# A two-layer hybrid diffusion trunk on one core: the first norm and its products by quarters of the features, a fourth raw slot, the norm's squares by halves, and the last rows in two transfers

## The chip, the cores and the metric

The kernel runs on one NeuronCore of a Trainium2 chip. The metric is the device time of one execution in microseconds (us). The kernel before took 1372.78 us, the median of three runs (1372.05 to 1373.74).

## The reference, cut to what matters

One inference step of a backbone of two layers (`DEPTH` = 2, `D_MODEL` = 1024) in float32 on 640 tokens: 512 latent tokens (`x_sample`) and 128 context tokens (`x_prompt`). Context and latent tokens share the weights and are modulated by different vectors (`c_ctx` and `c`). A layer is:

```
m = silu(cond) @ w_ada + b_ada                  # six vectors of 1024: shift, scale, gate, twice
h = rmsnorm(x, g_pre_mix) * (1 + scale1) + shift1
pa_u, pa_v, pb_h, pb_b, pb_c, pc, pd = split(h @ w_in)       # 1888 columns; pd has 352 of them
mix = concat(chunk_mlp(pa), short_conv(pb), fourier(pc), latent_attention(pd)) @ w_out
x = x + gate1 * rmsnorm(mix, g_post_mix)
h2 = rmsnorm(x, g_pre_ffn) * (1 + scale2) + shift2
x = x + gate2 * rmsnorm(swiglu(h2, w_gate_up, w_down), g_post_ffn)
```

Outputs are `y_prompt`, `y_sample` and, for each layer, the context's normalised latents and rotary keys. The change lies in the first three lines of the first layer (their scale and shift, the norm and the 352 columns `pd`), in the norms, and in the storing of the last rows.

## The kernel before, in words

**Numbers and tiles.** The 640 tokens are five tiles of 128 (tiles 0 to 3 latent, tile 4 context). Products that need float32 accuracy are made as three matmuls of float32r operands (`mm3`, lines 227 to 229): high part by high part, high by low, low by high. So an operand is split once (`split`, lines 211 and 217): ScalarE copies the high part, rounded, and VectorE subtracts it from the source for the low part. A weight goes from memory to one of three `raw` slots (pool `rp`, 4 KB a partition each), is split into one of eight `w` slots (pool `wp`), and the raw slot is free again when VectorE has read it (`load`, line 255). Other pools are `qp` (twelve large slots), `sp` (three small slots, tag `s`), `mp` (small tiles by tag) and eight PSUM banks (`ps`).

**The order of the work.** The program is traced once, in the order of the Python code, and a scheduler then orders each engine's queue by the program's order and by what is ready in its own estimate; slots of a pool are given in that order, and a tile with no free slot waits for a release. DMA issues stand in SP's queue. Where a block stands under `manual_schedule`, the engines it names keep the order written. Beside this, the kernel has a clock of its own, `now`, which each matmul advances by its estimated length (`clk`): generators (`spawn`) yield a time, and their next part is written into the program when the clock has come that far; background steps (`bg`: the modulations of later stages, with loads of 512 KB through `raw`) are written in at fixed distances. These distances are unchanged.

**The start** (`start`, line 1291). The first modulation, scale and shift of 1024 features for two conditions, is a product of two condition columns with 8 MB of `w_ada`. It is made in two halves of 512 features. A half has four blocks of 1 MB, loaded into `qp` slots (`fetch`, line 1300); for each block TensorE makes four matmuls side by side in groups of 32 columns (`ada_mm`, line 284, eight passes in the profile), and when all four are in, `fin` copies the sums out of PSUM (ScalarE), turns them by four transposes, and adds them, the bias and the norm's weight into `mod` (VectorE). The five tiles of x are loaded and normed meanwhile (`normalise`): ScalarE squares and sums a row of 1024 (line 432), GpSimd adds epsilon and takes the power -0.5, VectorE scales the row by halves (line 435). Then, for each half of the features, four transposes a tile bring the features onto the partitions (`xnT`, line 240), `modulate` applies scale and shift out of PSUM, two blocks of 128 on ScalarE and two on VectorE (lines 211 and 464), and `split_h` splits 512 columns into `h`. The products of `pd` (`pd`, 352 columns, eight feature blocks k, three matmuls each) run in two passes over the five tiles, k 0 to 3 and then k 4 to 7, in five PSUM banks `acc`. The steps of the second half's modulation stand between the products of the first pass. The weights `w_pd` are four loads of 352 KB, two blocks k each.

**Behind it.** `pd_chain` norms the two low-rank parts of a tile of `pd` in the tile `pdt` (one slot, lines 678 to 697), waits for 6.0 of the kernel's clock, transposes it and splits the result. `mixer` follows with its own weights (`w_vpc` first, four loads), and `w_out`, `gate_up` and `w_down`; the second layer's first norm and its 352 columns are made at the end of the first layer's `w_down` by `prenorm` and `pd_all`, not by `start`. Rows of a finished tile are updated by `postnorm` in two halves (line 914). At the end of the last layer `end(t)` stores them to `y_s` or `y_p` in one transfer of 512 KB (line 1199); tile 2 is the last.

## Time and profile before

| what | value |
|---|---|
| median of 3 runs | 1372.78 us (1372.05 to 1373.74) |
| the profiled execution, its own time | 1373.93 us |
| its span | 1372.2 us |
| TensorE (PE) busy | 1331.6 us, 97% of the span, 8188 matmuls |
| VectorE (DVE) busy | 1031.7 us, 75% |
| ScalarE (ACT) busy | 694.4 us, 51% |
| GpSimd (POOL) busy | 218.5 us, 16% |
| moved by DMA | 244.08 MB |

Times in the rows below are in us from the span's start. PE is TensorE's matmuls, PEld its weight loads, DVE VectorE, ACT ScalarE, POOL GpSimd, SPq the queue from which SP issues DMAs. "L227" is line 227 of the kernel; a helper's line stands for all its callers, so groups are told apart by the tiles, written out<-in. Idle time of an engine is put down to what released it, with "<-"; a DMA is given as its target and source. A matmul's end is modelled, so matmuls that follow each other overlap in the rows.

### The profile page before, as it was taken

What the parts mean: (1) busy time and instruction counts of PE and PEld (TensorE: products, weight loads), DVE (VectorE), ACT (ScalarE), POOL (GpSimd) and SP (SyncE); (2) the same over time, 40 slices, a digit from 0 to 9 for tenths busy, and PEclk for the clock granted to TensorE, in tenths of its full rate; (3) what the DMA queues carried; (4) which work ended last, traced back from release to release, by engine and by line L of the source; (5) the groups of instructions that cost most, each with busy time, mean ns of one, the idle gap of its engine ahead of it and who ended that gap; (6) DMA issues with size and microseconds to landing.
All of it is one profiled execution on the core that took longest, in us unless ns stands there. A gap on an engine that the chain in (4) does not pass through costs nothing. (4 is left out here: it accounts for less than half of the span.)

```text
span 1372.2 us, 21590 instructions
## 1 busy us (share of the span) xinstructions
PE 1331.6 (97%) x8188; PEld 1200.3 (87%) x8188; DVE 1031.7 (75%) x1794; ACT 694.4 (51%) x1398; POOL 218.5 (16%) x306
## 2 busy tenths in 40 slices
PE   5899999999999999999999999999999999999997
PEld 2789977899999999988888997878999999998886
DVE  3789476589979976868788966757976877776875
ACT  4543276465454444656583324736545444554652
POOL 1101121111122112100121202301223112210010
PEclk9999999999999999999999999999999999999999
DMA  9555247345778567746565633554279665655653
GB/s 373 177 168 188 80 148 246 107 154 177 254 201 231 191 168 201 207 143 188 175 207 175 191 113 123 185 200 168 73 238 229 186 160 149 167 131 155 182 182 126
DMA packets 69688, 244.08 MB, mean 178 GB/s; under 512 B 8960, under 2 KB 9856, under 8 KB 68560
## 3 DMA queue, kind: packets, MB, share of 16 engines
q1 hardware_dynamic: 56272, 196.56, 42.6%
q0 software_dynamic: 13312, 46.14, 14.3%
q8 instruction: 64, 1.05, 0.3%
q14 instruction: 40, 0.33, 0.1%
HBM read 231.99 MB, written 56.82 MB: 210 GB/s over the span
## 5 line engine op out<-in xcount | busy, mean ns | idle before, releaser
L227 PE MATMUL ps<-T,w 128*128 128x320 f32 x640 | 198.5, 310 | 1.3 <-DVE s L214 1.3
L229 PE MATMUL ps<-T,w 128*128 128x320 f32 x640 | 197.8, 309 | 0.0
L228 PE MATMUL ps<-T,w 128*128 128x320 f32 x640 | 197.7, 309 | 0.0
L211 ACT ACTIVATE w<-raw 128x1024 fp32r<-128x1024 f32 (+3 forms) x148 | 147.1, 1000 | 95.1 <-DMA raw<-in_w_b 39.6
L217 DVE TENSOR_TENSOR w<-raw,w 128x1024 fp32r<-128x1024 f32 (+3 forms) x148 | 170.4, 1155 | 29.9 <-ACT w L211 29.4
L227 PE MATMUL ps<-b,w 128*128 128x320 f32 x608 | 188.0, 309 | 0.0
L229 PE MATMUL ps<-b,w 128*128 128x320 f32 x608 | 187.9, 309 | 0.0
L228 PE MATMUL ps<-b,w 128*128 128x320 f32 x608 | 187.9, 309 | 0.0
L227 PE MATMUL ps<-w,hs 128*128 128x512 f32 x396 | 154.4, 390 | 0.1
L228 PE MATMUL ps<-w,hs 128*128 128x512 f32 x396 | 154.1, 389 | 0.0
L229 PE MATMUL ps<-w,hs 128*128 128x512 f32 x396 | 153.9, 389 | 0.0
L211 ACT ACTIVATE w<-wk 128x512 fp32r<-128x512 f32 x120 | 74.9, 628 | 107.0 <-PE ps L229 97.1
L217 DVE TENSOR_TENSOR w<-sw,w 128x512 fp32r<-128x512 f32 x160 | 106.0, 686 | 29.8 <-ACT w L211 28.3
L211 ACT ACTIVATE s<-ps 128x320 f32<-128x320 f32 (+2 forms) x148 | 65.5, 443 | 114.6 <-PE ps L229 94.6
L227 PEld LDWEIGHTS ps<-T,w 128*128 128x128 f32 x640 | 120.1, 188 | 3.7 <-DVE s L214 2.0
L228 PEld LDWEIGHTS ps<-T,w 128*128 128x128 f32 x640 | 120.2, 188 | 0.0
L229 PEld LDWEIGHTS ps<-T,w 128*128 128x128 f32 x640 | 120.1, 188 | 0.0
L214 DVE TENSOR_TENSOR s<-ps,s 128x320 f32<-128x320 f32 (+1 forms) x144 | 68.5, 482 | 64.6 <-PE ps L229 63.1
L228 PEld LDWEIGHTS ps<-b,w 128*128 128x128 f32 x608 | 114.1, 188 | 0.1
L227 PEld LDWEIGHTS ps<-b,w 128*128 128x128 f32 x608 | 114.1, 188 | 0.1
L229 PEld LDWEIGHTS ps<-b,w 128*128 128x128 f32 x608 | 114.1, 188 | 0.0
L211 ACT ACTIVATE w<-sw 128x512 fp32r<-128x512 f32 x160 | 95.2, 622 | 28.5 <-PE ps L229 27.7
(238 smaller groups left out, 2982.2 us busy)
## 6 DMA issues: line engine op xcount, KB each, us to landing
raw<-in_ada SPq DMA_DIRECT2D x80, 512.0 KB, 4.2
wk<-in_w_gu SPq DMA_DIRECT2D x80, 512.0 KB, 4.6
v<-in_w_dn POOLq DMA_DIRECT2D x60, 512.0 KB, 7.3
raw<-v SPq DMA_DIRECT2D x40, 512.0 KB, 3.5
raw<-in_w_dn SPq DMA_DIRECT2D x30, 512.0 KB, 3.9
v<-v POOLq DMA_DIRECT2D x20, 512.0 KB, 5.0
ada<-in_ada SPq DMA_DIRECT2D x8, 1024.0 KB, 11.9
raw<-in_w_out SPq DMA_DIRECT2D x16, 512.0 KB, 4.3
```

Source lines behind the costliest of these rows:

```text
L211: self.nc.scalar.activation(out, in_, f, **kw)
L214: self.nc.vector.tensor_tensor(out, x, y, op=op)
L217: self.nc.vector.tensor_tensor(lo, src, hi.bitcast(F32), op=ALU.subtract)
L227: mm(out, lh, rh, start=start, stop=False, skip_group_check=more)
L228: mm(out, lh, rl, start=False, stop=False, skip_group_check=more)
L229: mm(out, ll, rh, start=False, stop=stop, skip_group_check=more)
```

## The change

The first modulation is made in quarters of 256 features in place of halves: the host lays `w_ada` out as four quarters of two blocks of 1 MB, which are loaded into `w` slots. The loads of the first two quarters are issued between the tiles of x and the first `w_pd`; the third quarter, each further `w_pd`, the fourth quarter and the tables of `mixer_start` follow. The transposed rows are copied out of PSUM for a whole tile at once (`transposed`, ScalarE and VectorE by halves), and `feature(t, q)` then applies scale and shift in SBUF to two blocks of 128, one on each engine, and splits 256 columns. The `pd` products run in four passes over the five tiles, two blocks k each. Up to the norm of tile 4 the order on ScalarE and VectorE is written out. The due times of the five low-rank chains are 6.0, 9.2, 12.4, 15.6 and 18.8 of the kernel's clock.

The tile `pdt` and the context rows `ctx` move to the three shared small slots, the bias columns `mcol` have one buffer a stage in place of two, and `rp` has four slots. Every norm (20 of them) squares its row by halves of 512 with two sums, which GpSimd adds. In the last layer each tile's rows are stored as two halves of 512 columns.

The removed lines of `start` stand in the listing above and are left out.

```diff
--- before.py
+++ after.py
@@ -79,7 +79,9 @@
-    o["ada0"] = np.stack([np.stack([np.concatenate([wa[0, 2 * kk + e, :, j] for e in range(2) for j in (hf, 2 + hf)], -1) for kk in range(4)]) for hf in range(2)])
+    first = wa[0].reshape(2, 4, 128, 12, 2, 256)
+    o["ada0"] = np.stack([np.concatenate([first[:, :, :, b + q // 2, q % 2] for b in (0, 2)], -1).transpose(0, 2, 1, 3).reshape(2, 128, 2048)
+                          for q in range(4)])
...
@@ -287,13 +289,13 @@
     def new_mod(self, l, r):
 
         mod = self.M([2, 8, 2], f"mod{r}", 2)
-        mc = self.M([48], f"mc{r}", 2)
+        mc = self.M([48], f"mc{r}", 1)
         self.nc.sync.dma_start(out=mc, in_=self.a["mcol"][l, r])
         return mod, mc
 
     def mod_scale(self, mod, mc, j):
         nc = self.nc
-        c = slice(4 * j.start, 4 * j.stop)
+        c = slice(int(4 * j.start), int(4 * j.stop))
...
@@ -428,9 +430,10 @@
 
     def normalise(self, work):
 
-        ms = self.M([1], "ms", 6)
-        self.act(work[:, 0:1024], work[:, 1024:2048], AF.Square, scale=1 / 32.0, accum_out=ms)
-        r = self.rsq(ms)
+        ms = self.M([2], "ms", 6)
+        for hf in range(2):
+            self.act(work[:, hf * 512 : hf * 512 + 512], work[:, 1024 + hf * 512 : 1536 + hf * 512], AF.Square, scale=1 / 32.0, accum_out=ms[:, hf : hf + 1])
+        r = self.rsq(ms, two=True)
         for hf in range(2):
             self.nc.vector.tensor_scalar(work[:, hf * 512 : hf * 512 + 512], work[:, 1024 + hf * 512 : 1536 + hf * 512], r, None, op0=ALU.mult)
 
@@ -542,7 +545,7 @@
         self.grow = dc[:, 1536:1856]
         chan = dc[:, 1856:2368]
         self.cols = dc[:, 2368:2380]
-        ctx = self.M([256], "ctx", 1)
+        ctx = self.S(256)
         nc.sync.dma_start(out=ctx, in_=a["ctx"][l])
 
 
@@ -556,7 +559,7 @@
         self.split(kv[:, 0, 512:640], kv[:, 1, 512:640], ctx[:, 0:128])
         nc.gpsimd.tensor_copy(krT[:, 512:640], ctx[:, 128:256])
         self.st = (ql, kv, krT, kp, qp, pcp, Vp, chan)
-        self.chain = lambda t, ps: self.spawn(self.pd_chain(l, t, ps, cs, ql, kv, krT, kp))
+        self.chain = lambda t, ps, wait=6.0: self.spawn(self.pd_chain(l, t, ps, cs, ql, kv, krT, kp, wait))
 
     def more_pd(self, l):
         self.wpd += [self.load(self.a["w_pd"][l, u], cols=704) for u in range(2, 4)]
@@ -672,10 +675,10 @@
                     self.split(y67[:, 0, p, 0:512], y67[:, 1, p, 0:512], po[p])
         return [self.y01, y23, self.y45, y67], ctxt
 
-    def pd_chain(self, l, t, ps, cs, ql, kv, krT, kp):
+    def pd_chain(self, l, t, ps, cs, ql, kv, krT, kp, wait):
         nc, a, grow = self.nc, self.a, self.grow
         c = slice(t * 128, t * 128 + 128)
-        pt = self.M([448], "pdt", 1)
+        pt = self.S(448, "pdt")
         ms = self.M([2], "ms2", 2)
         self.act(pt[:, 0:192], ps[:, 0:192], AF.Square, scale=192.0 ** -0.5, accum_out=ms[:, 0:1])
         self.act(pt[:, 192:320], ps[:, 192:320], AF.Square, scale=128.0 ** -0.5, accum_out=ms[:, 1:2])
@@ -695,7 +698,7 @@
         if t == 4:
             nc.sync.dma_start(out=a["s_ckv"][l], in_=pt[:, 192:320])
             nc.sync.dma_start(out=a["s_kr"][l], in_=pt[:, 320:352])
-        yield 6.00
+        yield wait
         p2 = self.PS()
         self.tr(p2[0:96, 0:128], pt[:, 0:96])
         self.tr(p2[0:96, 128:256], pt[:, 96:192])
@@ -1196,7 +1199,9 @@
                 dst = nxt[2][t]
             else:
                 dst = a["y_p"] if t == 4 else a["y_s"][t * 128 : t * 128 + 128, :]
-            nc.sync.dma_start(out=dst, in_=xt)
+            for o in range(0, 1024, 1024 if nxt is not None else 512):
+                n = slice(o, 1024 if nxt is not None else o + 512)
+                nc.sync.dma_start(out=dst[:, n], in_=xt[:, n])
 
 
         bA = [self.PS(), self.PS()]
@@ -1293,73 +1298,122 @@
         a, nc = self.a, self.nc
         mod, mc = self.new_mod(0, 0)
...
+        psa, raws = {}, []
+        def fetch(q, i):
+            w = self.W()
+            nc.sync.dma_start(out=w, in_=a["ada0"][q, i])
+            raws.append(w)
+        def step(q, i):
+            if i == 0:
+                psa[q] = self.PS()
+            w = raws.pop(0)
+            self.ada_mm(psa[q], [(4 * i + j, w[:, j * 512 : j * 512 + 512]) for j in range(4)], i == 0, i == 1)
+        def fin(q):
+            pv = self.ada_cols(psa.pop(q))[:, :, :, 0:2]
             m = self.M([4, 2, 2], "modo", 2)
             nc.vector.tensor_copy(m, pv[:, :, 2:4, :])
+            self.tt(m, pv[:, :, 0:2, :], m, ALU.add)
             for kind in range(2):
...
+                v = m[:, 2 * kind : 2 * kind + 2]
+                self.tt(mod[:, kind, 2 * q : 2 * q + 2], v[:, :, 0], v[:, :, 1], ALU.add)
+            self.mod_scale(mod, mc, slice(q / 2, (q + 1) / 2))
         works = [self.Q([2048], F32, "work") for _ in range(NT)]
...
+        h = self.new_h()
+        acc = {}
+        self.wpd = []
+        def wpd(u):
+            self.wpd.append(self.load(a["w_pd"][0, u], cols=704))
+        def transposed(t):
+            for jj in range(2):
+                ps = self.xnT(works[t], jj)
+                o = works[t][:, 1024 + 512 * jj : 1536 + 512 * jj]
+                if jj:
+                    nc.vector.tensor_copy(o, ps)
+                else:
+                    self.act(o, ps)
+        def feature(t, q):
+            s = 1 if t == 4 else 0
+            hf = works[t][:, 1024 + 256 * q : 1280 + 256 * q].rearrange("p (q n) -> p q n", q=2)
+            for c in range(2):
+                k = 2 * q + c
+                sc, sh = mod[:, 1, k, s : s + 1], mod[:, 0, k, s : s + 1]
+                if c:
+                    self.act(hf[:, c], hf[:, c], AF.Identity, scale=sc, bias=sh)
+                else:
+                    nc.vector.tensor_scalar(hf[:, c], hf[:, c], sc, sh, op0=ALU.mult, op1=ALU.add)
+            c = slice(t * 128, t * 128 + 128)
+            d = slice(2 * (q % 2), 2 * (q % 2) + 2)
+            self.split(h[q // 2][0][:, d, c], h[q // 2][1][:, d, c], hf)
+        def norm(t):
             self.normalise(works[t])
...
+        for f in (lambda: fetch(0, 0), 0, 1, lambda: fetch(0, 1), 2, "w", lambda: fetch(1, 0), 3, lambda: fetch(1, 1), 4):
+            if f == "w":
+                raw0 = self.raw()
+                nc.sync.dma_start(out=raw0[:, :704], in_=a["w_pd"][0, 0])
+            elif isinstance(f, int):
+                self.load_x(a["x"], f, works[f])
+            else:
+                f()
         with self.tc.manual_schedule(engines={mybir.EngineType.Activation, mybir.EngineType.DVE}):
+            step(0, 0)
+            norm(0)
+            norm(1)
+            transposed(0)
+            step(0, 1)
+            norm(2)
+            transposed(1)
+            fin(0)
+            feature(0, 0)
+            w = self.wp.tile([128, 2, 1024], R, tag="w", name=self.nm("w"))
+            self.split(w[:, 0, :704], w[:, 1, :704], raw0[:, :704])
+            self.wpd.append(w)
+            feature(1, 0)
+            transposed(2)
+            norm(3)
+            feature(2, 0)
+            norm(4)
+        for i in range(2):
+            fetch(2, i)
+        pds = []
+        for q in range(4):
             for t in range(NT):
...
+                if q == 0:
+                    acc[t] = self.PS()
+                    if t == 1:
+                        transposed(3)
+                    if t == 2:
+                        transposed(4)
+                if q < 3:
+                    if t == (2 if q == 0 else 0):
+                        step(q + 1, 0)
+                        step(q + 1, 1)
+                    if t == (3 if q == 0 else 1):
+                        fin(q + 1)
+                if t + 1 < NT and (q, t + 1) not in ((0, 1), (0, 2)):
+                    feature(t + 1, q)
+                self.pd(t, acc[t], h, (2 * q, 2 * q + 1))
+                if q < 3:
+                    if t == 0:
+                        wpd(q + 1)
+                    if t == 4:
+                        feature(0, q + 1)
+                        if q == 0:
+                            for i in range(2):
+                                fetch(3, i)
+                        if q == 1:
+                            self.mixer_start(0)
+                else:
+                    pds.append(self.chain(t, acc[t], 6.0 + 3.2 * t))
         return h, pds
     def run(self):
@@ -1407,7 +1461,7 @@
         tc.tile_pool(name="cp", bufs=1) as cp,
         tc.tile_pool(name="qp", bufs=12) as qp,
         tc.tile_pool(name="wp", bufs=8) as wp,
-        tc.tile_pool(name="rp", bufs=3) as rp,
+        tc.tile_pool(name="rp", bufs=4) as rp,
         tc.tile_pool(name="sp", bufs=3) as sp,
         tc.tile_pool(name="gp", bufs=2) as gp,
         tc.tile_pool(name="mp", bufs=1) as mp,
```

## Rows read from the trace of the kernel before

**Rows 1.** Waits of TensorE, whole span: us in total, times, longest.

```profile
PE ps L284 <- DMA ada<-in_ada: 11.2, 4, 7.1
...
PE ps L227 <- ACT w L211: 2.6, 2, 1.8
PE ps L240 <- DVE pdt L693: 2.6, 4, 1.0
```

**Rows 2.** Sums by stretch: window, its length, busy us (instructions), clock, DMA share, GB/s.

```profile
0.00:29.80 29.80, 13.91 (x57) 5.41 (x57) 7.75 (x24) 10.78 (x19) 4.78 (x14) 1.00 0.93 368
29.80:60.56 30.76, 28.22 (x180) 22.66 (x180) 22.65 (x51) 19.26 (x44) 2.76 (x5) 1.00 0.64 224
...
75.00:90.00 15.00, 15.00 (x68) 12.43 (x67) 11.94 (x14) 6.25 (x12) 0.00 (x0) 1.00 0.52 176
```

**Rows 3.** Timeline of the start: start, duration, what, [idle before <- releaser].

```profile
7.12 1.93 PE L284 MATMUL ps<-ada,cond 128*32 128x512 f32 x8 [7.12 <-DMA ada<-in_ada]
...
10.91 1.06 ACT L211 ACTIVATE work<-work 128x1024 f32<-128x1024 f32 x1 [6.90 <-DMA work<-in_x]
...
13.06 0.88 DVE L435 TENSOR_SCALAR work<-work,rt 128x512 f32<-128x512 f32 x2 [11.89 <-POOL rt L252]
...
13.61 1.12 PE L240 MATMUL ps<-ident,work 128*128 128x128 f32 x4 [2.01 <-DVE work L435]
...
17.09 1.54 ACT L211 ACTIVATE w<-raw 128x704 fp32r<-128x704 f32 x2
...
24.83 0.60 ACT L211 ACTIVATE s<-ps 128x512 f32<-128x512 f32 x1 [6.20 <-PE ps L284]
...
26.39 1.92 PE L240 MATMUL ps<-ident,work 128*128 128x128 f32 x8
...
27.58 0.81 ACT L211 ACTIVATE work<-ps,mod 128x128 f32<-128x128 f32 x2 [2.16 <-DVE mod L301]
...
29.80 0.43 PE L227 MATMUL ps<-w,h 128*128 128x352 f32 x1 [1.49 <-ACT h L211]
...
30.79 0.32 PE L227 MATMUL ps<-w,h 128*128 128x352 f32 x1
...
30.95 0.32 PE L228 MATMUL ps<-w,h 128*128 128x352 f32 x1
...
32.32 1.07 PE L284 MATMUL ps<-ada,cond 128*32 128x512 f32 x8
```

**Rows 4.** Groups by shape, 0 to 62 us: count | busy us, mean ns | idle before.

```profile
L211 ACT ACTIVATE work<-ps,mod 128x128 f32<-128x128 f32 x20 | 7.7, 460 | 3.2 <-DVE mod L301 3.2
...
L217 DVE TENSOR_TENSOR w<-raw,w 128x704 fp32r<-128x704 f32 x4 | 3.5, 888 | 0.1
```

**Rows 5.** Timeline, single instructions of the shapes that the change uses.

```profile
70.40 0.39 ACT L211 ACTIVATE v<-ps 128x256 fp32r<-128x256 f32 x1
...
72.56 0.41 DVE L217 TENSOR_TENSOR v<-ps,v 128x256 fp32r<-128x256 f32 x1
...
1347.28 0.64 ACT L211 ACTIVATE t<-cc 128x512 f32<-128x512 f32 x1 [0.89 <-DVE cc L214]
...
1347.91 0.58 ACT L211 ACTIVATE cc<-ps 128x512 f32<-128x512 f32 x1
...
1363.44 0.69 DVE L214 TENSOR_TENSOR work<-ps,gg 128x512 f32<-128x512 f32 x1 [9.38 <-ACT work L211]
```

**Rows 6.** Timeline, a stop for the low-rank tile and one for a weight.

```profile
61.60 0.42 PE L240 MATMUL ps<-ident,pdt 128*96 128x128 f32 x2 [1.04 <-DVE pdt L693]
...
897.46 1.06 ACT L211 ACTIVATE w<-raw 128x1024 fp32r<-128x1024 f32 x1 [3.41 <-DMA raw<-in_w_out]
```

**Rows 7.** Timeline, TensorE's longest stop for a norm's scaling behind the start.

```profile
713.49 0.77 PE L240 MATMUL ps<-ident,work 128*128 128x128 f32 x5 [1.84 <-DVE work L435]
```

**Rows 8.** The end: VectorE's last instruction (timeline), and the stretch behind it (sums).

```profile
1367.42 0.75 DVE L914 SCALAR_TENSOR_TENSOR work<-work,rt 128x512 f32<-128x512 f32 x1
...
1368.20:1370.00 1.80, 0.00 (x0) 0.00 (x0) 0.00 (x0) 0.00 (x0) 0.00 (x0) 0.50 0.57 230
```

More of the change, by code (lines that the diff above doesn't have):

```diff
@@ L1295, in start @@
         mod, mc = self.new_mod(0, 0)
-        psa, raws = [None, None], []
-        def fetch(half, kk):
-            q = self.Q([2048], F32, "ada")
-            nc.sync.dma_start(out=q, in_=a["ada0"][half, kk])
-            raws.append(q)
-        def step(half, kk):
-            if kk == 0:
-                psa[half] = self.PS()
-            q = raws.pop(0)
-            self.ada_mm(psa[half], [(2 * kk + j // 2, q[:, j * 512 : j * 512 + 512]) for j in range(4)], kk == 0, kk == 3)
-        def fin(half):
-            pv = self.ada_cols(psa[half])[:, :, :, 0:2]
+        psa, raws = {}, []
@@ L1313, in fin @@
             for kind in range(2):
-                self.tt(mod[:, kind, 4 * half : 4 * half + 4], pv[:, :, kind, :], m[:, :, kind, :], ALU.add)
-            self.mod_scale(mod, mc, slice(half, half + 1))
-        for kk in range(2):
-            fetch(0, kk)
+                v = m[:, 2 * kind : 2 * kind + 2]
+                self.tt(mod[:, kind, 2 * q : 2 * q + 2], v[:, :, 0], v[:, :, 1], ALU.add)
+            self.mod_scale(mod, mc, slice(q / 2, (q + 1) / 2))
         works = [self.Q([2048], F32, "work") for _ in range(NT)]
-        for t in range(NT):
-            self.load_x(a["x"], t, works[t])
@@ L1322, in start @@
-        self.first_pd(0)
-        for kk in range(2, 4):
-            fetch(0, kk)
-        for t in range(NT):
-            self.normalise(works[t])
-        for kk in range(4):
-            step(0, kk)
-        pss = {t: self.xnT(works[t], 0) for t in range(3)}
-        fin(0)
-        for kk in range(4):
-            fetch(1, kk)
-        h = self.new_h()
-        acc = []
-        def sink(t, jj, ps):
-            hf = works[t][:, 1024 + 512 * jj : 1536 + 512 * jj].rearrange("p (q n) -> p q n", q=4)
-            self.modulate(t, jj, ps, mod, hf, START[jj][t])
-            self.split_h(t, jj, h, hf)
@@ L1341, in start @@
-        with self.tc.manual_schedule(engines={mybir.EngineType.Activation, mybir.EngineType.DVE}):
-            for t in range(NT):
-                sink(t, 0, pss[t])
-                if t + 3 < NT:
-                    pss[t + 3] = self.xnT(works[t + 3], 0)
-        self.more_pd(0)
-        self.mixer_start(0)
-        for t in range(NT):
-            acc.append(self.PS())
-            self.pd(t, acc[t], h, range(4))
-            if t < 4:
-                step(1, t)
-            if t == 3:
-                fin(1)
@@ L1355, in start @@
-        pds = []
-        pss = {0: self.xnT(works[0], 1)}
-        for t in range(NT):
-            if t + 1 < NT:
-                pss[t + 1] = self.xnT(works[t + 1], 1)
-            sink(t, 1, pss[t])
-            self.pd(t, acc[t], h, range(4, 8))
-            pds.append(self.chain(t, acc[t]))
+        h = self.new_h()
[11 more added lines that the diff above has]
+                    self.act(o, ps)
```

## The prediction

> **What bounds the kernel now.** I read first the waits of TensorE over the whole span, then the sums by stretch, then the timeline of the first 75 us and of the last 10.
>
> The longest wait of TensorE is for the first modulation weights: 11.2 us in 4 stops [rows 1]. The sums by stretch place it: up to 29.80 us TensorE is busy for 13.91 us and the DMA engines for 93% [rows 2]; then the first product of the normalised input starts [rows 3]. From there to the last product of this group, at 60.56, TensorE is busy for 28.22 of 30.76, and from 75 to 90 throughout [rows 2]. So the kernel is bound by TensorE, except ahead of 29.80 us, where it is bound by the loads and what hangs on them. Smaller waits remain: 2.6 us for the low-rank chain's tile (line 693) and 2.6 us for weight splits (line 211) [rows 1], and stops for a norm's scaling (line 435), the longest 1.84 [rows 7]. After the last matmul nothing but the closing chain and one transfer is left, up to 1372.2 [rows 8].
>
> The profiled execution took 1373.93 us, 1.73 more than its span and 1.15 more than the median of the runs, 1372.78. I sum against it and take the 1.15 off at the end.
>
> **The start, step by step.** The first block of 1 MB lands at 7.12; the next block and the first rows of x, 1.5 MB, have landed at 10.91 [rows 3]. That is 2.53 us for a megabyte, 1.26 for 512 KB and 0.87 for 352 KB. Now the first product needs all four blocks of half a modulation, behind x and two loads of w_pd: ScalarE copies the sum at 24.83, the columns are usable at 27.58, and the product starts at 29.80 [rows 3]. The change loads the same 8 MB, but a quarter needs only two blocks, and they are spread among the rows of x. Landings by these rates: block 7.1, x0 8.4, x1 9.6, block 12.2, x2 13.4, w_pd 14.3; second quarter 16.8 and 20.6, with x3 at 18.1 between and x4 at 21.9 behind; third quarter 24.4 and 26.9; w_pd 27.8; fourth quarter 30.3 and 32.9; w_pd 33.7; tables 36.9; w_pd 37.8.
>
> First product, by the order that the change writes out for ScalarE and VectorE. From the square of tile 0 to the end of its scaling it takes 3.03 now (10.91 to 13.06 + 0.88) [rows 3]. A square of half the columns costs 0.63 to the next instruction (1347.28 to 1347.91) [rows 5], so two cost 0.2 more than one of 1.06, and the scaling ends at 8.4 + 3.2 = 11.6. Eight transposes at 1.92 (26.39) give 13.5, the second step 1.93, as the first took [rows 3], 15.4. Half of tile 1's transposes (1.0) and their copy (0.58 [rows 5]) stand ahead of the step's own copy: 17.0. From that copy's start to usable columns it is 2.75 (24.83 to 27.58): 19.8. One feature block on ScalarE (0.46 [rows 4]), its split (0.39 and 0.41 for 256 columns [rows 5]), and behind them the split of w_pd, 0.77 on ScalarE [rows 3], 0.89 on VectorE [rows 4], partly side by side: 21.5, which I take. Ends: 20.6 without VectorE's half on the path, 23 if tile 2's norm pushes in.
>
> Behind the first product TensorE has the same 120 products. One lasts 0.32, but they overlap and start 0.16 apart (30.79, 30.95) [rows 3], 19 us in all. Four modulation steps lie behind it before and after (the second half; the third and fourth quarter). Transposes are 24 before (20 of x, 4 of columns) and 36 after (24 and 12). Twelve more at 0.12 to 0.24 are 1.5 to 2.9; I take 1.5, since they fall in the stream. So 28.22 + 1.5 = 29.7 busy. Idle I take as 1.5, between 0 and 2.54 (what it is now): tile 4's scaling ends at about 30 (from 21.5: block 0.85, copy 0.58, tile 3's norm 3.2, block 0.85, tile 4's norm 3.2), and the second w_pd is split at 29.5; till then TensorE has tiles 0 to 3 of the first quarter and the steps of the second and third. End of the products: 21.5 + 31.2 = 52.7 against 60.56, **7.9 us** gained.
>
> What could be late next: the last w_pd lands at 37.8, its split takes 1.7, a quarter's products 4.8: 44.3, so the loads do not bind. ScalarE has 24.7 us of work behind 21.5 (20 blocks at 0.85 less the first, 16.2; two norms 2.6; three tiles' copies 1.8; columns 1.8; three w_pd 2.3) and would be done at 46.2. VectorE is near that; a block of 128 columns from SBUF is not in the trace there. Its ends are 0.11 (a quarter of the 0.44 for 512 columns at 13.06 [rows 3]) and 0.46 (ScalarE's block [rows 4]); I take 0.27, midway, since one is the same engine and the other the same size. Both stay below 52.7, with 5 us or so to spare. Ends of this term: 10.9 (first product at 20.6, idle 0, and 0.6 fewer for transposes done earlier) and 3.5 (first rival).
>
> **The other parts.** *Low-rank chain.* Its tile had one buffer, so that each chain waited for the transposes of the one before; at 61.60 TensorE stood for 1.04 for it [rows 6]. The tile now comes from three shared slots, and the due times are 3.2 apart. I take 1.5 of the 2.6 [rows 1]; ends +1.0 (one more such stop, when a shared slot is held) and -2.6. The context rows move to these slots too: nothing, their load lies beside the products. The single mcol buffer: nothing, its second use is hundreds of us later.
>
> *Fourth raw slot.* At 897.46 ScalarE had stood 3.41 for an output projection's load [rows 6], and TensorE for the split. A load is issued when the slot's last split is done, so a further slot moves the load ahead by one split: 0.77 and 0.89 for 704 columns [rows 3, 4], 2.4 for 1024. TensorE's longest such stop is 1.8 [rows 1]. I take 1.5 of the 2.6; ends -2.6 and +1.0 (loads that run ahead share the DMA engines with those that are due; a third of 3.41).
>
> *Squares by halves.* 20 norms of 0.2 more on ScalarE are 4 us; they lie beside TensorE, as ScalarE is busy for half the span; uncovered they would cost 4. Where TensorE waits for a norm [rows 7], the first square may start when half the rows are updated, 0.75 earlier (a half's update, [rows 8]), so that the second ends 0.4 earlier. Two such stops: I take 0.8; ends -1.1 and +0.4.
>
> *Rows in two transfers.* VectorE ends at 1368.17 and the span 4.0 later [rows 8]. Half the bytes take 0.63 less by the rate above, and the first half's issue lies beside the second half's 0.75. I take 0.5; ends 0.4 (one more issue in the way) and -0.63.
>
> Sum: 7.9 + 1.5 + 1.5 + 0.8 + 0.5 = 12.2; 1373.93 - 12.2 = 1361.7, less 1.15, **1360.6 us**. The best ends give 10.9 + 2.6 + 2.6 + 1.1 + 0.6 = 17.8, 1355.0; the worst 3.5 - 1.0 - 1.0 - 0.4 - 0.4 = 0.7, 1372.1.
>
> **Rivals.** *TensorE stands behind tile 4.* Its queue runs in order: at 61.60 it stood for a transpose with products behind it [rows 6]. If tile 4's transposes, ready at 30, are queued ahead of the second quarter's steps and of what is left of the first quarter's products, 4.4 us of work slip and the products end at 57: 3.5 gained, 4.3 elsewhere, 1365.0. For it: these transposes stand early in the program. Against: TensorE's order before is not the program's either, the transposes at 13.61 [rows 3] ran ahead of the third and fourth step, which stand first in the program and whose blocks were late.
>
> *Given back.* VectorE is busy for 11.94 of 15 us from 75 to 90 [rows 2], and the start gets more for it: ten copies out of PSUM at 0.69 [rows 5] are 6.9. If the splits of the next weights fall behind, TensorE stands for them, and half of the start's 7.9 is lost: 1364.6; if the quarters' loads come in the old order as well, because SP's issues are held up by slots, all of it: 1368.5. For it: the little spare. Against: the splits are issued as early as before, and TensorE did not stand in that stretch.
>
> *Slower: the products run at half clock.* Place: the four quarters, where TensorE may stop between bursts. The same eight passes took 1.93 at 7.12, after 7 us without work, and 1.07 at 32.32 in the stream [rows 3], while the granted clock reads 1.00 (2.4 GHz) in both stretches [rows 2]; behind the last matmul it reads 0.50, 1.2 GHz [rows 8]. Price: half rate costs 0.15 for each product, 18 for 120: less the 12.2 that makes 5.8 slower, 1378.6. It decides from 81 products (12.2 / 0.15). For it: shorter bursts. Against: the products at 29.80 came after 1.49 of idle and were 0.16 apart within a microsecond [rows 3]. The Trainium skill (TensorE: Matmul & The Clock Gate, Part 1: The HAM clock gate) says that half rate is the default, that activity releases it and that idling brings it back. The doubled lengths agree with it, though the clock column does not show it there; by this rule the time would be the rival's if the quarters leave TensorE idle for long.
>
> **Chances.** Forecast 0.61; tile 4 0.16; given back 0.12; half clock 0.05; other 0.06. The range is 1355 to 1369.5: the forecast's own ends, the first rival and nearly all of the second. A difference of 0.2% (2.7 us) is about what the measurement can tell from no change, so faster is under 1370.0. Faster: nearly all of the forecast and of tile 4 (0.76), most of given back (0.08), half of the other: 0.87. Same 0.07, slower 0.06.
>
> **What would show it.** Right: first product at 20 to 23 us, last at 50 to 55, landings as listed, no stop for line 693 at the end of the products, under 1 us of waits for w_out's splits, 3.4 us from VectorE's end to the span's. Wrong: products 0.30 apart (clock); a stop of TensorE over 3 us between 21 and 31 (tile 4); waits for splits of w_vpc behind the products (given back); new waits over 2 us after 90, where I expect the order of the work to stay.

## The result, and the profile after

| | before | after |
|---|---|---|
| median, us (9 runs each, same chip) | 1373.74 | 1367.30 (1363.28 to 1371.01) |
| ratio, 95% interval | | 0.9945 [0.9929, 0.9961] |
| profiled execution, us; its span | 1373.93; 1372.2 | 1365.13; 1363.4 |
| first product of the normalised input | 29.80 | 21.24 |
| end of the last product of layer 1's `v` | 92.35 | 89.34 |
| end of the last `w_out` product, layer 1 / layer 2 | 284.69 / 953.32 | 280.80 / 944.53 |
| end of the last `w_down` product, layer 2 | 1364.72 | 1356.42 |

Faster by 7.5 us (5.4 to 9.8), where 12.2 were forecast. The last three rows are starts plus durations of the last instruction of each kind in the timelines, of one profiled execution each. The `v` products (512 columns, `w_vpc`) follow those of `pd`; in the new kernel the two mix, since the first `v` product starts at 53.63 while the last `pd` product ends at 61.31, so the end of `v` is the mark by which the start is judged; how far it moves by itself is shown ahead of the experiments. The first product came 8.56 us earlier, and of that 3.01 were left at the end of `v`; 8.3 of gain stood at the last matmul all the same, so more than half came from behind the start.

Lines of the new kernel are two to three higher: L286 is the old L284, L229 to L231 the old L227 to L229, L242 the old L240, L213 and L219 the old L211 and L217, L438 the old L435, L917 the old L914. Waits of TensorE, whole span (us in total, times, longest), answering to [rows 1]:

```profile
PE ps L242 <- DVE work L438: 8.9, 6, 3.1
PE ps L286 <- DMA wk<-in_ada: 7.4, 1, 7.4
...
PE ps L229 <- ACT w L213: 2.0, 1, 2.0
```

The four stops for modulation blocks are one, and no line for `pdt` is left. The first place is taken by the norm's scaling (L438), with a stop of 3.1. Timeline of the start (start, duration, what, [idle before <- releaser]), answering to [rows 3]:

```profile
7.37 1.94 PE L286 MATMUL ps<-wk,cond 128*32 128x512 f32 x8 [7.37 <-DMA wk<-in_ada]
...
15.08 1.93 PE L286 MATMUL ps<-wk,cond 128*32 128x512 f32 x8
...
19.56 0.49 ACT L213 ACTIVATE work<-work,mod 128x128 f32<-128x128 f32 x1 [1.89 <-DVE mod L303]
...
20.41 0.77 ACT L213 ACTIVATE w<-raw 128x704 fp32r<-128x704 f32 x1
...
21.24 0.43 PE L229 MATMUL ps<-w,h 128*128 128x352 f32 x1 [1.98 <-ACT w L213]
...
22.91 0.32 PE L231 MATMUL ps<-w,h 128*128 128x352 f32 x1
22.91 0.42 DVE L219 TENSOR_TENSOR h<-work,h 128x256 fp32r<-128x256 f32 x1 [0.55 <-ACT h L213]
...
25.66 0.88 DVE L438 TENSOR_SCALAR work<-work,rt 128x512 f32<-128x512 f32 x2 [1.72 <-POOL rt L254]
...
26.29 1.94 PE L242 MATMUL ps<-ident,work 128*128 128x128 f32 x8 [3.05 <-DVE work L438]
...
28.91 0.49 PE L229 MATMUL ps<-w,h 128*128 128x352 f32 x1
29.20 0.49 PE L230 MATMUL ps<-w,h 128*128 128x352 f32 x1
...
30.61 0.88 DVE L438 TENSOR_SCALAR work<-work,rt 128x512 f32<-128x512 f32 x2 [1.06 <-POOL rt L254]
...
31.15 1.97 PE L242 MATMUL ps<-ident,work 128*128 128x128 f32 x8 [1.17 <-DVE work L438]
33.05 2.68 PE L286 MATMUL ps<-wk,cond 128*32 128x512 f32 x16
...
35.93 0.32 PE L230 MATMUL ps<-w,h 128*128 128x352 f32 x1
36.09 0.32 PE L231 MATMUL ps<-w,h 128*128 128x352 f32 x1
```

After six products TensorE stands for 3.05 us: next in its queue are tile 3's transposes, whose norm VectorE scales only at 25.66. Tile 1's products, whose split ends at 23.33, stand behind them. Tile 4's transposes follow in the same way (1.17). The second quarter's steps (33.05, sixteen passes) are queued behind both. And from 26.29 on the same work takes double: transposes 1.94, products 0.29 apart, until they are 0.16 apart again at 36.09. The sums by stretch (window, its length, busy us (instructions) of PE, PEld, DVE, ACT, POOL, clock, DMA share, GB/s), answering to [rows 2], with the stretch behind the last VectorE instruction for [rows 8], say why:

```profile
0.00:21.24 21.24, 9.01 (x45) 4.97 (x45) 6.00 (x21) 8.75 (x21) 3.13 (x10) 1.00 0.87 347
...
21.24:89.34 68.10, 62.80 (x338) 50.13 (x339) 53.59 (x131) 39.89 (x108) 7.11 (x15) 0.92 0.59 214
...
24.40:34.60 10.20, 7.14 (x30) 5.24 (x34) 4.58 (x11) 4.99 (x15) 1.72 (x4) 0.50 1.02 408
...
75.00:90.00 15.00, 15.00 (x75) 12.51 (x74) 14.77 (x20) 8.10 (x18) 0.00 (x0) 1.00 0.57 182
...
1359.90:1361.50 1.60, 0.00 (x0) 0.00 (x0) 0.00 (x0) 0.00 (x0) 0.00 (x0) 0.50 0.88 328
```

From 24.40 to 34.60 the granted clock is 0.50, 1.2 GHz. Two more views: groups by shape from 0 to 62 us (count | busy us, mean ns | idle before), answering to [rows 4], and VectorE's last instruction.

```profile
L1351 DVE TENSOR_SCALAR work<-work,mod 128x128 f32<-128x128 f32 x20 | 5.9, 343 | 0.1
...
L213 ACT ACTIVATE work<-work,mod 128x128 f32<-128x128 f32 x20 | 9.1, 486 | 6.9 <-DVE mod L303 6.9
```

```profile
1359.11 0.75 DVE L917 SCALAR_TENSOR_TENSOR work<-work,rt 128x512 f32<-128x512 f32 x1
```

From its end, 1359.86, to the end of the span are 3.5 us, where there were 4.0 [rows 8].

### The profile page after: what moved, and what is told of

It reads as the page before. It is cut to its first block, busy times and chain, and to the rows that moved or that the text cites. A ratio compares the mean times of both kernels' runs of the same rounds, so it can differ in the third digit from the quotient of the medians.

```text
span 1363.4 us, 21724 instructions
## 1 busy us (share of the span) xinstructions
PE 1330.5 (98%) x8196; PEld 1203.4 (88%) x8196; DVE 1037.0 (76%) x1825; ACT 702.5 (52%) x1455; POOL 220.1 (16%) x306
## 4 chain that ended last, share of the span: by engine, by line
PE 72%; DVE 10%; issue 8%; DMA 5%; POOL 2%; ACT 2%; SPq 0%; POOLq 0%; DVEq 0%; ACTq 0%
PE ps L229 22%; PE ps L231 22%; PE ps L230 22%; DVE acc L379 3%; PE ps L242 3%; DMA wk<-in_w_gu 2%; PE ps L286 2%; DVE w L219 2%; DMA raw<-in_ada 2%; POOL rt L254 1%; PE ps L829 1%; DVE s L216 1%; POOL rs L250 1%; DVE sw L216 1%; ACT w L213 1%
## 5 line engine op out<-in xcount | busy, mean ns | idle before, releaser
L229 PE MATMUL ps<-T,w 128*128 128x320 f32 x640 | 198.8, 311 | 3.1 <-DVE s L216 3.1
L231 PE MATMUL ps<-T,w 128*128 128x320 f32 x640 | 197.9, 309 | 0.0
L229 PE MATMUL ps<-b,w 128*128 128x320 f32 x608 | 188.2, 309 | 0.0
L231 PE MATMUL ps<-b,w 128*128 128x320 f32 x608 | 188.0, 309 | 0.0
L219 DVE TENSOR_TENSOR w<-raw,w 128x1024 fp32r<-128x1024 f32 (+3 forms) x148 | 169.2, 1152 | 23.7 <-ACT w L213 23.4
L213 ACT ACTIVATE w<-raw 128x1024 fp32r<-128x1024 f32 (+3 forms) x148 | 146.7, 999 | 58.6 <-DMA raw<-in_w_b 22.8
L229 PE MATMUL ps<-w,hs 128*128 128x512 f32 x396 | 154.5, 390 | 0.1
L231 PE MATMUL ps<-w,hs 128*128 128x512 f32 x396 | 154.0, 389 | 0.0
L219 DVE TENSOR_TENSOR w<-sw,w 128x512 fp32r<-128x512 f32 x160 | 106.4, 687 | 31.9 <-ACT w L213 30.6
L213 ACT ACTIVATE w<-wk 128x512 fp32r<-128x512 f32 x120 | 75.1, 627 | 99.8 <-PE ps L231 96.1
L229 PEld LDWEIGHTS ps<-T,w 128*128 128x128 f32 x640 | 120.2, 188 | 6.1 <-DVE s L216 4.4
L213 ACT ACTIVATE s<-ps 128x320 f32<-128x320 f32 (+2 forms) x150 | 66.5, 445 | 108.3 <-PE ps L231 96.4
L231 PEld LDWEIGHTS ps<-T,w 128*128 128x128 f32 x640 | 120.2, 188 | 0.0
L229 PEld LDWEIGHTS ps<-b,w 128*128 128x128 f32 x608 | 114.2, 188 | 0.1
L231 PEld LDWEIGHTS ps<-b,w 128*128 128x128 f32 x608 | 114.2, 188 | 0.0
L213 ACT ACTIVATE w<-sw 128x512 fp32r<-128x512 f32 x160 | 95.7, 623 | 31.5 <-PE ps L231 27.6
```

The source lines that it names most:

```text
L213: self.nc.scalar.activation(out, in_, f, **kw)
L219: self.nc.vector.tensor_tensor(lo, src, hi.bitcast(F32), op=ALU.subtract)
L229: mm(out, lh, rh, start=start, stop=False, skip_group_check=more)
L231: mm(out, ll, rh, start=False, stop=stop, skip_group_check=more)
```

## The experiments

Ratios are against runs of the kernel before on the same chip, five rounds each.

**How far the start moves by itself.** Two of the runs below leave the order of the start as it is in the change: the one with three raw slots, and the one with whole squares. Their profiles differ from the change's all the same. With three slots the second step took 1.07 (15.04) where it had taken 1.93, the first product came at 20.34, tile 3's stop was 2.71 and tile 4's 1.33. The clock fell ahead of tile 3's stop and not in it, and was back at 1.00 by 28.7. The sum by stretch there, which holds about 6.8 us of half clock in place of 10.2:

```profile
21.60:28.60 7.00, 4.29 (x18) 3.87 (x17) 3.39 (x8) 4.55 (x14) 0.86 (x2) 0.51 1.02 412
```

The end of `v` was 86.87 there and 85.87 with whole squares. So this order gives marks from 85.87 to 89.34, and an edit whose mark lies among them has shown nothing by it.

**The second quarter's steps first.** The two steps go ahead of the loop, so that TensorE meets them before tile 3's transposes.

```diff
+        step(1, 0)
+        step(1, 1)
         for q in range(4):
...
-                    if t == (2 if q == 0 else 0):
+                    if q > 0 and t == 0:
```

> The changed kernel with the two modulation steps of the second quarter written ahead of the first product instead of behind tile 4's transposes. Theory A (TensorE's queue runs in order; the steps, whose blocks land at about 17 and 21 us, stood behind transposes that were ready at 26.3 and 31.2): the steps move into the stop ahead of the first product, the 2.68 us that they took at 33.05 go, and the end of the v products comes 2.5 to 4 us earlier than the 89.34 of the changed kernel; the whole is 2.5 to 4 us faster than it. Rival B (the loads or ScalarE set the pace of the quarters): the end of the v products stays within 0.7 us. The stop for tile 3's transposes (3.05) stays in both.

Measured: 0.9941 [0.9920, 0.9963], not told apart from the change (0.9945). In the profile the stops are 2.63 and 1.35, and the end of `v` comes at 86.84, 2.50 before the changed kernel's. That is the low end of what theory A expected, but level with the 86.87 that came with the steps left where they were, so it is not shown to come from the edit.

```profile
21.60:25.60 4.00, 1.38 (x9) 0.80 (x6) 1.73 (x5) 2.99 (x8) 0.86 (x2) 1.00 1.02 424
25.60:29.00 3.40, 3.39 (x14) 3.25 (x14) 1.80 (x5) 2.27 (x7) 0.05 (x1) 0.50 1.03 406
29.00:36.00 7.00, 5.65 (x44) 4.53 (x46) 4.89 (x17) 3.54 (x8) 1.11 (x3) 1.00 1.02 406
```

In these sums by stretch the half clock lasts 3.4 us, where it was 10.2 and 6.8 with the steps behind. Both steps now run ahead of the stop, at 18.50 and 20.91, the first of them in time in which TensorE had nothing else to do. The stop for tile 3 stays, 0.42 shorter: what it waits for has to come earlier.

**The stop filled.** Twenty-four transposes of no use for the result stand where TensorE waited.

```diff
                 self.pd(t, acc[t], h, (2 * q, 2 * q + 1))
+                if q == 0 and t == 0:
+                    ps = self.PS()
+                    for i in range(24):
+                        nc.tensor.transpose(ps[:, i % 4 * 128 : i % 4 * 128 + 128], self.wpd[0][:, 1, 0:128].bitcast(F32), self.ident)
```

> The changed kernel with 24 transposes of no use behind the first tile's first products, where TensorE stopped for 3.05 us; nothing is removed. Theory C (the stop let the granted clock fall to 0.50 at 24.39, and the work up to 34.63 was paid at half rate): the clock stays at 1.00 over that stretch, tile 3's transposes take 1.0 to 1.1 instead of 1.94, the products behind them start 0.16 apart instead of 0.29, and the end of the v products comes 2.5 to 4 us earlier than 89.34, though TensorE has 3 us more to do. Rival (the half rate costs nothing since the work was late anyway): the end stays within 0.7 us, or comes later by what the added work takes.

Measured: 0.9905 [0.9883, 0.9927], 0.40% under the change, though 24 transposes are added. The timeline of TensorE and a sum by stretch:

```profile
23.32 4.45 PE L1408 MATMUL ps<-ident,w 128*128 128x128 f32 x24
27.60 1.04 PE L242 MATMUL ps<-ident,work 128*128 128x128 f32 x8
```

```profile
23.70:27.00 3.30, 3.30 (x17) 3.30 (x16) 1.58 (x4) 1.52 (x5) 0.86 (x2) 0.50 0.98 404
27.10:40.00 12.90, 12.00 (x90) 8.41 (x89) 8.65 (x26) 9.31 (x23) 1.16 (x3) 1.00 1.02 398
```

The stop is filled, and the half clock ends at 27 and not at 34.6 (28.6 with three slots, unfilled): tile 3's transposes take 1.04, not 1.94. It was not kept away: it came while TensorE was busy with the added work, behind the stops of 1.98 and 0.50 at the first products. The end of `v` is 87.06, 2.28 earlier than in the change (2.5 to 4 were expected) and no earlier than 86.87 with the stop left empty. So the profile does not show that the filling moved the start, nor that idling cost more than useless work in its place. The ratio is better by 5.5 us, its interval just clear of the change's; of the 4.4 by which the profiled span is shorter, 2.1 came behind `v`, and their source was not followed.

**Norms first (e4).** What the stop waits for is brought ahead: the scalings of tiles 3 and 4 are written ahead of the features of tiles 1 and 2. The second quarter's steps go ahead too, as in the first experiment.

```diff
             fin(0)
+            step(1, 0)
+            squares(3)
             feature(0, 0)
...
             self.wpd.append(w)
+            step(1, 1)
+            scale(3)
+            squares(4)
             feature(1, 0)
             transposed(2)
-            norm(3)
+            scale(4)
             feature(2, 0)
-            norm(4)
```

(`squares` and `scale` are the two halves of `normalise`; the loop leaves the second quarter's steps out, and `fin(1)` comes one tile earlier.)

> The changed kernel with the steps of the second quarter ahead of the first product, and with the squares of tiles 3 and 4 moved ahead on ScalarE (into its wait for the first columns), their scalings behind the split of the first w_pd. Nothing else differs. If the order written out for ScalarE and VectorE made tiles 3 and 4 late: no stop over 1 us behind the first product, the clock at 1.00 from about 18 us on, the end of the v products 5 to 7 us earlier than 89.34, near what was forecast for the start (7.9 earlier than 92.35 less its 1.8 of chain stops), and 5 to 7 us faster than the changed kernel. If ScalarE or VectorE bounds the quarters: new waits for feature blocks or splits, less than 3 us gained.

Measured: 0.9904 [0.9881, 0.9928], 5.6 us under the change, end of `v` 82.17: about as expected, but for a stop of 1.24. Two stretches and TensorE's only stop over 0.2 between its first product and 51:

```profile
20.99:51.38 30.39, 28.86 (x189) 23.40 (x190) 24.63 (x78) 24.88 (x68) 3.38 (x7) 1.00 0.78 306
...
20.99:82.17 61.18, 58.74 (x330) 47.77 (x331) 53.30 (x131) 38.17 (x104) 7.41 (x13) 1.00 0.65 239
```

```profile
25.52 0.43 PE L229 MATMUL ps<-w,h 128*128 128x352 f32 x1 [1.24 <-ACT h L213]
```

The clock stays at 1.00; the products end at 51.38 with 28.86 busy and 1.53 idle. The forecast had 29.7, 1.5 and 52.7: its sum fits this order, not the one that was written. It had counted four steps and 36 transposes behind the first product; here they are five and 28, in the change six and 28. The end of `v` is 3.70 earlier than the earliest of the old order and 4.67 earlier than with the steps alone, so the place of the norms did move it. The other cure, tile 3's transposes further back in TensorE's queue, was not tried. The ratio alone would not tell: the filled stop has the same (0.9905), with `v` ending 4.89 later.

**Three raw slots.** The change with `rp` at 3 again.

> The changed kernel with three raw slots again. If the fourth slot is what took the stops for w_out's splits away: stops of 1.8 and 1.4 us at the start of w_out are back, and where the one of the second layer lasts, a stretch at half clock behind it, so 2 to 5 us slower than the changed kernel, all of it in w_out. If the earlier start of everything did it: no stop there, within 1 us of the changed kernel.

Measured: 0.9987 [0.9967, 1.0007]: without the fourth slot the change is worth nothing that can be told. The end of `v` is at 86.87, but first `w_out` at 225.50 (222.51 with four). Against the change with four slots, 5.46 us are lost between these two marks. One of its stops, in the convolution's products, and the stretch behind it:

```profile
123.25 0.42 PE L229 MATMUL ps<-h,w 128*128 128x320 f32 x1 [1.89 <-DVE ua L724]
```

```profile
124.30:127.50 3.20, 3.07 (x13) 2.88 (x13) 3.20 (x6) 2.81 (x6) 0.00 (x0) 0.50 0.40 146
```

Others stand at 513.3 (1.94), 794.1 (2.02) and 900.4 (0.97). So the slot is worth 0.0042, 5.8 us, and not at `w_out` alone, as I had expected: of the stops there only the one of 0.97 is back. Which stops are the missing slot's is not shown: with four slots the second layer's convolution also had stops of 1.99 (steps first) and 2.05 (stop filled), without half clock behind them.

**The fourth raw slot alone.** The kernel before with four raw slots, `pdt` and `ctx` in the shared small slots and one `mcol` buffer, which make room for the slot; the start as before.

> The kernel before with the fourth raw slot, and with what makes room for it (the low-rank tile and the context rows in the shared slots, one mcol buffer); the start, the norms and the stores as before, due times of the chains all 6.0. By the three-slot run (which was 0.42% behind the changed kernel in its ratio to before) the fourth slot is worth 5 to 6 us wherever the start is: 4 to 7 us faster than before, the stops of w_out gone, no half-clock stretch near 899. By the forecast's term (1.5 for the slot and up to 1.5 for the low-rank tile): 1.5 to 3 us faster, within the noise of one run. If the slot pays only together with the earlier start: within 1 us of before.

Measured: 0.9959 [0.9938, 0.9980], 5.6 us; no stop for `pdt`, none at layer 2's `w_out`. No stretch near 899 is at half clock. In its profile it is 2.33 behind the kernel before at the end of the first layer's `w_out` (287.02) and 4.67 ahead at the second's (948.65), so the gain stands between them. A second reading of the slot, with the chain's tile, of the same size. Which share is the chain's was not tried.

**Halves and rows alone.** The kernel before with the squares by halves and the rows in two transfers.

> The kernel before with squares by halves and the last rows in two transfers, nothing else. Forecast: 0.8 + 0.5, so 1.3 us faster, of which 0.4 to 0.6 stand between VectorE's last instruction and the span's end (4.0 before), and the two stops for a norm's scaling (1.47 and 1.84) are 0.3 to 0.5 shorter each. Rival: 20 norms of 0.2 us on ScalarE reach TensorE, and it is 1 to 4 us slower.

Measured: 0.9976 [0.9953, 0.9998], 3.3 us with an interval from 0.3 to 6.5. Of the named stops the one at 294 went from 1.47 to 0.68, the one at 712 from 1.84 to 1.80, neither by the expected 0.3 to 0.5.

```profile
715.93 1.09 PE L240 MATMUL ps<-ident,work 128*128 128x128 f32 x8 [1.80 <-DVE work L436]
...
1369.51 0.75 DVE L915 SCALAR_TENSOR_TENSOR work<-work,rt 128x512 f32<-128x512 f32 x1
```

The timeline of VectorE ends at 1370.26 and the span at 1373.5: 3.2 for 4.0. The two shown effects make 1.6. But this profiled execution is 1.3 longer than the one before (1372.2): its first products, from 29.73 to 33.3, ran at half rate, 0.29 apart, and `v` ended at 95.90, 3.55 later, though the order of the start is the old one. So the 3.3 us are not found in the profile.

**The same two edits undone in the change.**

> The changed kernel with the norm's squares of whole rows and the last rows in one transfer, as before; quarters, slots and chains as changed. By the forecast's terms (0.8 and 0.5) it is 1.3 us slower than the changed kernel: ratio 0.9954, with 0.5 of it behind VectorE's last instruction (4.0 in place of 3.5). By the measurement of these two edits alone (ratio 0.9976) 3.3 us slower: 0.9969. Rival: in the start the halves cost more than they give (two squares of 0.63 in place of one of 1.06 for five norms in the way of the first products): first product 0.3 to 0.6 earlier than 21.24 and the whole no slower than the changed kernel, 0.994 to 0.9945.

Measured: 0.9931 [0.9908, 0.9954], not told apart from the change: neither 1.3 us (0.9954, at the interval's end) nor 3.3 (0.9969) is borne out. VectorE ended at 1360.63 and the span at 1364.6, 4.0 as expected, so the two transfers' 0.5 is read a second time. The first product came at 20.04, as the rival had it and by more, but mostly for another reason:

```profile
14.74 1.06 PE L286 MATMUL ps<-wk,cond 128*32 128x512 f32 x8
...
24.83 1.94 PE L242 MATMUL ps<-ident,work 128*128 128x128 f32 x8 [2.44 <-DVE work L437]
```

The second step took 1.06 where the changed kernel's took 1.93, which is 0.87 of the 1.20; the step starts 0.34 earlier, and that is what the whole squares can have given. The run with three slots bears it out: halved squares, a step of 1.07, first product at 20.34, so 0.30 is left for the squares. The stop for tile 3 is there (2.44).

**Norms first with three raw slots.**

> The order of e4 (tile 3's and tile 4's norms ahead) with three raw slots in place of four. If the fourth slot is a term of its own, it costs here what it cost in the changed kernel (ratio 0.9987 with three slots against 0.9945 with four, 0.0042): 0.9904 + 0.0042 = 0.9946, last v product at 82 to 83, about 10 us ahead of the kernel before, and half of that lead lost by the first w_out product. If instead three slots give back whatever the start gains, since the weights behind the start then arrive too late for an earlier start, the ratio comes out at 0.997 to 1.001 again, and the lead of about 10 us at the last v product is under 3 us at the first w_out product of the first layer.

Measured: 0.9918 [0.9887, 0.9948]. The interval just reaches the first theory's 0.9946 and not the second's 0.997. The end of `v` at 82.22 is 10.13 ahead of before, first `w_out` 217.96 is 6.14 ahead: 4 of 10 us given back, against 1.2 with four slots (215.08). At the end of the span 1.0 is left of it (1358.6 against 1357.6). So in the profile three slots give back part of an early start. By the ratio the slot is worth 0.0014 here, and the interval reaches 0.0042 as well: whether the slot adds a fixed sum to any start stays open.

**Norms first, TensorE busy early (e7).** Sixteen transposes of the identity ahead of the first block and eight of tile 0's raw rows behind the first step, all of no use for the result.

```diff
+            ps = self.PS()
+            for i in range(16):
+                nc.tensor.transpose(ps[:, i % 4 * 128 : i % 4 * 128 + 128], self.ident[:], self.ident)
             step(0, 0)
+            ps = self.PS()
+            for i in range(8):
+                nc.tensor.transpose(ps[:, i % 4 * 128 : i % 4 * 128 + 128], works[0][:, 1024:1152], self.ident)
```

> The kernel with the norms of tiles 3 and 4 first, and with 16 transposes of the identity ahead of the first modulation block and 8 of unscaled rows behind it, all of no use, where TensorE was idle. If the start's path is paid at half clock (16 transposes took 3.68 and the second step 1.93 there): the granted clock reaches 1.00 by about 12 instead of 16 us, tile 0's and tile 1's transposes and the second step take half, the first product starts at 18.5 to 19.5 instead of 20.99, and the whole is 1 to 2.5 us faster than the norms-first kernel. If ScalarE's and VectorE's order sets the first product, or the clock rises no earlier: within 0.7 us of it.

Measured: 0.9878 [0.9841, 0.9915]. The steps ahead of the first product ran at full rate from the first on (1.07 at 7.43), but the first product came at 21.19, not earlier:

```profile
18.28 0.63 ACT L213 ACTIVATE work<-work 128x512 f32<-128x512 f32 x1 [2.36 <-DMA work<-in_x]
...
19.53 0.48 ACT L213 ACTIVATE work<-work,mod 128x128 f32<-128x128 f32 x1
...
21.19 0.66 PE L229 MATMUL ps<-w,h 128*128 128x352 f32 x1 [1.98 <-ACT w L213]
```

ScalarE stood for tile 3's rows and squared them first, as written. Behind the first product the clock then stood at 0.50:

```profile
21.10:24.50 3.40, 3.31 (x12) 1.35 (x13) 1.94 (x4) 0.75 (x3) 0.00 (x0) 0.50 1.02 424
```

The end of `v`, 83.53, is 1.36 later than without the fill, and the ratio is not told apart from 0.9904.

**The same with tile 3's squares behind the split of `w_pd`.**

> As e7 (its added transposes too, of no use for the result), but tile 3's two squares stand behind the first feature block and the split of w_pd on ScalarE. In e7 the first modulation was ready at 18.47, but ScalarE waited 2.36 us for tile 3's rows and squared until 19.53, and only then began the first feature block (0.48, 0.42, 0.77): first product 21.19. If this order is what kept the early fill from moving the first product, the block begins at about 18.5 and the first product at 20.1 to 20.4; tile 3's scaling moves from 21.97 to about 23, the last product to about 51 and the whole to a ratio of 0.986 to 0.989 (0 to 1 us below e7). Rival: what sets the first product is the landing of w_pd or the clock, and it stays at 21.0 to 21.5.

Measured: 0.9848 [0.9812, 0.9885], the lowest ratio of all, from four executions, of which the profiled one is the slowest (1362.49).

```profile
18.52 0.49 ACT L213 ACTIVATE work<-work,mod 128x128 f32<-128x128 f32 x1 [2.64 <-DVE mod L303]
...
20.20 0.42 PE L229 MATMUL ps<-w,h 128*128 128x352 f32 x1 [1.03 <-ACT w L213]
```

The block starts 1.01 earlier and the first product 0.99, as expected; the last product ends at 50.93, `v` at 81.70. ScalarE's written order had hidden what the fill gave: without the fill (e4) the columns were usable only at 19.12 and the block began at 19.33, so there the order cost 0.2 at most. Of the fill's own effect not all repeats: the first step took 1.83 here (7.41), 1.07 in e7. Against e7's ratio the difference is inside the intervals.

## Why the forecast was right, and where not

**Right: that the change is faster, and the first product.** 21.24 against 21.5, with the steps for it: tile 0's scaling ends at 11.82 (11.6), the column copy begins at 17.08 (17.0), columns usable at 19.5 (19.8). One feature block on VectorE took 0.34 (0.27 was taken), on ScalarE 0.49 (0.46). That 21.24 falls so near 21.5 holds for an execution whose second step took 1.93, as was taken; with 1.07 the same order gave 20.34.

**Wrong: "Idle I take as 1.5".** This is the step that failed, with its reason "till then TensorE has tiles 0 to 3 of the first quarter and the steps of the second and third". The times in it were good: tile 3's scaling ended at 26.54 (26.1 by the sum given there), tile 4's at 31.49 (30). But TensorE's queue had tile 3's transposes behind six products, and the steps behind tile 4's. The sum was also at odds with this reason: it counted four steps behind the first product, while the reason keeps the second quarter's two there as well. Six stood there, and 28 transposes for 36, errors that in part cancel.

From the first product to the end of `v` the changed kernel took 68.10, of which 5.30 idle; with the norms first 61.18, of which 2.44. The difference, 6.92, is 2.86 of idle and 4.06 of busy time. One step, which now runs ahead of the first product, is 1.07 of the latter (330 matmuls for 338); for the other 3.0 there is the half clock, since 7.14 us of work would take 3.6 less at full clock. The forecast's end of `v` is 52.7 + 31.79 (60.56 to 92.35 before) - 1.76 (the chain's stops in it) = 82.7: 6.6 early for the change (4.1 by the profile with three slots), 0.6 late for the norms first.

The first rival named this mechanism, for tile 4; tile 3's stop was the larger, and I had not looked for it. Its sign, a stop of over 3 us between 21 and 31, came, and the last `pd` product ended at 61.31, not between 50 and 55. Its 3.5 us for the start and 1365.0 for the whole are also nearer to what was measured (3.01 and 1367.30) than the forecast's 7.9 and 1360.6. The third rival's mechanism, the clock, took its part in it, for ten microseconds (6.8 with three slots) and not for 120 products.

The rule of the Trainium skill (TensorE: Matmul & The Clock Gate, Part 1: The HAM clock gate) that idling brings half rate back agrees with the 0.50 that begins inside the stop of 3.05. The same section warns that the trace's clock events can't be trusted one by one; here the column reads 1.00 at 15.08, where eight passes took 1.93, so lengths decide.

**Undersized: the fourth raw slot, 1.5.** In the profiles the stops for splits at `w_out` went (0.88, 0.53 and 1.76, together 3.17), and with the last of them a price that I had not counted. The sums by stretch of the kernel before, behind it:

```profile
897.00:899.10 2.10, 0.53 (x2) 0.48 (x3) 0.55 (x1) 1.64 (x3) 0.00 (x0) 1.00 0.80 246
899.30:902.50 3.20, 3.07 (x7) 2.15 (x7) 2.51 (x4) 2.12 (x2) 0.00 (x0) 0.50 0.52 152
902.70:906.00 3.30, 3.30 (x16) 2.69 (x15) 2.05 (x2) 1.06 (x1) 0.00 (x0) 1.00 0.95 374
```

3.07 busy at 0.50 cost 1.5 more, 4.7 in all; taking the slot away from the change cost 5.8 and adding it to the kernel before, with the chain's tile, gave 5.6. Where the rest lies was not isolated. Three slots lost 5.46 us against four between the end of `v` and the first `w_out` in the change, 2.83 with the norms first.

**The small terms.** The chain's four stops of 2.56 are all gone (1.5 taken). Rows in two transfers gave 0.49 (0.5). Of the norms' stops 1.47 became 0.50, and 1.84 became 0.55 + 1.52: 0.7 (0.8), which the runs with and without the halves neither confirm nor refute. Summed by the profiles: 1.25 for the start (3.01 less the chain's 1.76), 2.56, 4.7, 0.7 and 0.49 make 9.7; the span is 8.80 shorter. The 0.9 between was not followed; elsewhere stops came and went (0.91 at 218, 1.45 at 395, 0.92 at 1058; 0.95 at 126 gone). So the forecast's sum missed by less than its parts: the start fell short by 6.6, the slot and the chain gave 4.3 more. That the whole came inside the range is in part luck: these two errors, of opposite sign, stand against a forecast gain of 12.2. All these parts are read from one execution of each kernel.

**Given back** did not happen with four slots: at the end of the convolution's products 2.78 of the 3.01 were left, although VectorE was busy for 14.77 of the 15 us from 75 to 90 (11.94 before). With three slots it did: 5.48 ahead at the end of `v`, 1.40 behind at the first `w_out`. The rival put ten copies out of PSUM on VectorE; it makes five of them, ScalarE the others.

## What to carry to other kernels

When a stage is split finer, write down each engine's queue as the program will order it and set the ready time of every entry beside it: one early transpose whose input is late holds all that stands behind it. Price a stop of TensorE at more than its length: look in the granted clock for the stretch behind it. Read the marks of a start from more than one execution: the same order ended 2.5 us apart here. And judge a further load buffer together with the start that it serves: with three slots 4 of 10 us of an earlier start were lost again ahead of `w_out`.

## What the runs showed of the hardware that was not expected

- A stop of 3.05 us came with 10.2 us at 0.50, which began inside it; one of 2.63 was followed by 3.4, one of 1.76 by 3.2; the stops at the first products, 1.98 and 0.50, by 3.3 although TensorE was kept busy right behind them. But a stop of 2.02 in the second layer's convolution was followed by 3.3 (796.8 to 800.1, three slots), while 1.99 and 2.05 at the same place (steps first, stop filled) were followed by none.
- The same eight passes at the same place took 1.93 or 1.07 with the same order of the start (15.08 in the change, 15.04 with three slots), with 1.00 in the clock column in both.
- One execution of the change took 1363.28 and another 1371.01: edits worth under 3 us could not be told apart here, even in five rounds.
